# A decoder block on one core: the position bias as straight-line code with one conditional behind it

## The chip, the cores and the metric

The kernel runs on one core of one Trainium2 chip. The metric is the device time of one execution in microseconds (us). The kernel before takes 893.34 us, the median of three runs (891.0 to 894.33). TensorE does the matmuls, VectorE and ScalarE the elementwise work, GpSimd some of it, and SyncE starts most transfers; ScalarE starts the others, from its own queue.

## The reference

The reference is one decoder block over 512 tokens of width 1024: sparse attention with a T5 position bias beside a retention branch, gated and merged, then a layer norm, a squared-ReLU MLP of width 4096 and a second layer norm. What matters here is the bias of the attention: each query row keeps the 128 best keys by an indexer's score, and the logits of 8 heads get a bias that depends only on the distance of the two positions, by 32 buckets.

```python
def t5_bucket(rel):
    n = jnp.maximum(rel, 0)
    max_exact = NUM_BUCKETS // 2
    nf = jnp.maximum(n, 1).astype(jnp.float32)
    large = max_exact + (jnp.log(nf / max_exact) / math.log(MAX_DISTANCE / max_exact)
                         * (NUM_BUCKETS - max_exact)).astype(jnp.int32)
    large = jnp.minimum(large, NUM_BUCKETS - 1)
    return jnp.where(n < max_exact, n, large)
...
        bias = rel_bias[t5_bucket(posb[:, :, None] - pos_g)]
        logits = (jnp.einsum('bqhd,bqkhd->bqhk', qb, k_g).astype(jnp.float32) * (dh ** -0.5)
                  + bias.astype(jnp.float32).transpose(0, 1, 3, 2))
```

`positions` is an input. In the data that is timed it is 0, 1, 2, ..., 511; a kernel has to hold for others too.

## The kernel before

Every large product is done in full precision by three TensorE passes over a high and a low part (`mm3`, L142 to L147). A weight unit of 256 x 512 numbers is loaded by SyncE (`load_unit`, L124, four buffers), ScalarE casts its high part (`split_hi`, L132, three buffers), VectorE subtracts to get the low part (`split_lo`, L139, three buffers), and `group` runs the matmuls of the unit, 24 for each of the main projections. Each of these instructions stands in the queue of its engine; within a queue the order is fixed when the program is built. The builder walks through `main`, and at each `yield` of `group` (every 12 matmuls) calls `tick`, which advances the small tasks that are woven in between: rotary tables, indexer, top-k (L560, L561, on VectorE), the loads of the bias and the addition of the mask to it (`bm_task`, L578, L580), attention (`attn_task`, L617 to L657), retention. A planner then orders the instructions of each straight stretch of the program; a conditional ends a stretch, on all engines.

The order of the main projections is: indexer (8 units of a smaller kind, 8 ticks), attention keys (ticks 9 to 16), queries (17 to 24), values (25 to 32), then retention queries and keys with the rotary evacuation (`rope_evac`, L670, L673), and the rest.

The bias is made in three steps. `bias_by_distance` (L349) makes a row `R8` in DRAM, 8 heads by 640 distances. `bias_even` (L367) copies it, for positions that go up by one, into a DRAM tensor `bd[j]` for each of four blocks of 128 queries, 128 shifted copies of a row in one transfer. `bm_task` reads tiles of `bd` from there. For other positions `bias_general` computes every bias from its distance: `bias_prep` (VectorE) and 32 `bias_task`s (one-hot tables on VectorE, 12 matmuls each, ScalarE, a transfer). `bias_tables` finds out which case it is, a number `uneven` (L310), and `bias` (L328) holds the conditional at L333. It is called twice, behind the keys with heads 0 to 3 and behind the queries with heads 4 to 7; only the second call has the other arm.

```python
        uneven = self.nc.values_load(self.uneven[0:1, 0:1])
        with tc.If(uneven == 0) as cmp:
            self.bias_even(hs)
        if hs.stop == H:
            with cmp.Else():
                self.bias_general()
            self.flags.add("bias")
```

Of the kernel before, what the change touches and what calls it, by code (L numbers as in the profile page):

```python
# [11 lines left out]
F32 = mybir.dt.float32  # L12
F32R = mybir.dt.float32r
BF16 = mybir.dt.bfloat16
# [5 lines left out]
P = 128  # L20
# [3 lines left out]
H = 8  # L24
# [35 lines left out]
class Build:  # L60
# [67 lines left out]
    def split_hi(self, i):  # L128
        if i >= len(self.units) or i in self.whi:
            return  # L130
        hi = self.w.tile([P, *self.units[i][1:]], F32R, tag="whi", name=f"whi{i}", bufs=3)
        self.nc.scalar.copy(hi, self.raw[i])  # L132
        self.whi[i] = hi

    def split_lo(self, i):
# [122 lines left out]
    def setup_small(self):  # L258
        nc, d, sm = self.nc, self.d, self.sm
        self.cst = sm.tile([P, 160], F32, name="cst")  # L260
        nc.sync.dma_start(self.cst, d["cst"])
        self.posq = sm.tile([P, 4], I32, name="posq")
        nc.sync.dma_start(self.posq, d["posq"])
        self.posn = sm.tile([P, 4], I32, name="posn")
        nc.sync.dma_start(self.posn, d["posn"])
        self.posk = self.alloc(dt=I32, name="posk")
        nc.sync.dma_start(self.posk, d["positions"].to_broadcast([P, S]))
        self.mhalf = sm.tile([P, 16], F32, name="mhalf")
        nc.vector.memset(self.mhalf, -0.5)
# [19 lines left out]
    def bias_tables(self):  # L289
# [5 lines left out]
        for i in range(3):  # L295
            nc.vector.tensor_copy(parts[:, i], rb[:, i])
            if i < 2:
                nc.vector.tensor_sub(rb[:, i + 1], rb[:, i], parts[:, i])
        self.rbd = sm.tile([P, 3, 4, H], BF16, name="rbd")
        nc.vector.memset(self.rbd, 0.0)  # L300
        for q in range(4):
            r = slice(32 * q, 32 * q + 32)
            nc.vector.tensor_copy(self.rbd[r, :, q, :], parts[r])
        step, odd = self.alloc(shape=(1, S), dt=I32, name="step"), self.alloc(shape=(1, S), name="odd")
        n = S - 1
        nc.gpsimd.tensor_tensor(step[:, :n], self.posk[0:1, 1:], self.posk[0:1, :n], op=OP.subtract)
# [18 lines left out]
        return bass.AP(tensor=t.tensor, offset=t.offset + h * (P * w + P) + q * w + P - 1,  # L325
                       ap=[[w, nq], [P * w + P, nh], [1, n]])

    def bias(self, hs):  # L328


        tc = self.tc
        uneven = self.nc.values_load(self.uneven[0:1, 0:1])
        with tc.If(uneven == 0) as cmp:  # L333
            self.bias_even(hs)
        if hs.stop == H:
            with cmp.Else():
                self.bias_general()
            self.flags.add("bias")

    def bias_general(self):  # L340
        run, todo = [], [self.bias_prep()] + [self.bias_task(j, G) for j in range(NS) for G in range(8)]
        while run or todo:
            if todo:
                run.append(todo.pop(0))
            for g in list(run):
                if next(g, self) is self:
                    run.remove(g)

    def bias_by_distance(self):  # L349

# [4 lines left out]
        for i, sl in enumerate((slice(0, S), slice(S, W))):  # L355
            n = sl.stop - sl.start
            nc.sync.dma_start(bk[i][:, :n], self.d["buckets"][:, sl].to_broadcast([P, n]))
            nc.vector.tensor_scalar(oh[i][:, :n], bk[i][:, :n], self.bucket, None, op0=OP.is_equal)
            ps = self.ps.tile([P, S], F32, tag="s", name="tps", bufs=3)
            for p in range(3):  # L360
                nc.tensor.matmul(ps[:H, :n], lhsT=self.rbd[:, p, 0, :], rhs=oh[i][:, :n],
                                 start=p == 0, stop=p == 2)
# [4 lines left out]
    def bias_even(self, hs):  # L367

        for j in range(NS):
            w = self.pitch(j) + 1  # L370
            row = self.R8[hs, S - P * (j + 1):S - P * (j + 1) + w]
            src = bass.AP(tensor=row.tensor, offset=row.offset, ap=[[0, P], row.ap[0], row.ap[1]])
            self.nc.scalar.dma_start(self.bd[j][hs, :P * w].rearrange("h (q w) -> q h w", q=P), src)

    def bias_prep(self):

        nc = self.nc
        self.nd = []
        for j in range(NS):
            K = P * (j + 1)  # L380
            dn = self.alloc(dt=I32, name="dn")
            nc.gpsimd.tensor_tensor(dn[:, :K], self.posq[:, j:j + 1].to_broadcast([P, K]),
                                    self.posk[:, :K], op=OP.subtract)
            nv = self.allocs(2, name="nv")
            n, v = nv[0][:, :K], nv[1][:, :K]
            nc.vector.tensor_scalar(n, dn[:, :K], 0.0, NMAX, op0=OP.max, op1=OP.min)
            nc.vector.tensor_scalar(v, n, 1.0, None, op0=OP.max)
            nc.scalar.activation(v, v, AF.Ln, scale=0.0625)
            nc.vector.tensor_scalar(v, v, 16 / math.log(8), -0.49, op0=OP.mult, op1=OP.add)
            nc.vector.tensor_scalar(v, v, MAGIC, MAGIC - 1, op0=OP.add, op1=OP.max)  # L390
            nc.vector.tensor_scalar(v, v, MAGIC - 1, None, op0=OP.subtract)
            nb = self.alloc(dt=BF16, name="nb")
            nc.vector.scalar_tensor_tensor(nb[:, :K], n, 15.0, v, op0=OP.min, op1=OP.add)
            nd = self.dr.tile([P, K], BF16, name=f"nd{j}")
            nc.sync.dma_start(nd, nb[:, :K])
            self.free(dn, nb, nv)
            self.nd.append(nd)
            yield

    def bias_task(self, j, G):  # L400

        nc = self.nc
        K, C = P * (j + 1), P * j + 16 * (G + 1)
        while len(self.nd) <= j:
            yield
        yield from self.need(4)
        st = self.allocs(2, shape=(P, 2, K), dt=BF16, name="bst")
        for i in range(2):
            src = self.nd[j][16 * G:16 * G + 16, :].rearrange("(q g) k -> q g k", q=4)
            src = src[:, 2 * i:2 * i + 2].rearrange("q g k -> q (g k)")  # L410
            nc.sync.dma_start(st[i].rearrange("p g k -> p (g k)"),
                              src[:, None, :].to_broadcast([4, 32, 2 * K]))
        yield
        yield
        oh = self.allocs(2, shape=(P, 2, C), dt=BF16, name="boh")
        for i in range(2):
            nc.vector.tensor_scalar(oh[i], st[i][:, :, :C], self.bucket, None, op0=OP.is_equal)
        self.free(st)
        yield
        ps = self.ps.tile([P, S], F32, tag="s", name="bps", bufs=3)  # L420
        for p in range(3):
            for g in range(4):
                nc.tensor.matmul(ps[32 * g:32 * g + 32, :C],
                                 lhsT=self.rbd[:, p].rearrange("p q h -> p (q h)"),
                                 rhs=oh[g // 2][:, g % 2, :], start=p == 0, stop=p == 2)
        self.free(oh)
        ev = self.alloc(name="bev")
        nc.scalar.copy(ev[:, :C], ps[:, :C])
        if C < K:
            nc.gpsimd.memset(ev[:, C:K], 0.0)  # L430
        yield
        nc.sync.dma_start(self.bias_at(j, 0, H, 16 * G, 16, K), ev[:, :K])
        self.free(ev)


    def rope_prep(self):
# [351 lines left out]
    def main(self):  # L788
# [23 lines left out]
        for k in range(8):  # L812
            if k < 2:
# [10 lines left out]
        nc.vector.tensor_scalar(self.mask[0], self.causal, -1e38, NEG, op0=OP.is_lt, op1=OP.mult)  # L824
        self.flags.add("mask0")
        self.queue([self.rope_prep()], delay=14)
        self.queue([self.bm_task(j, 2 * i + p) for i in range(4) for j in range(NS) for p in range(2)],
                   1.0, 32)

# [17 lines left out]
        tb = [(P * i, P) for i in range(4)]  # L847
        self.kaT = self.allocs(4, name="kaT")
        yield from self.group(4, xT, tb, ev_copy(self.kaT, 1.0, "ka"), True)
        self.bias(slice(0, 4))  # L850
        self.qaT = self.allocs(4, name="qaT")
        yield from self.group(4, xT, tb, ev_copy(self.qaT, 0.125, "qa"), True)
        self.bias(slice(4, 8))
        self.free(self.posk)

        self.va = [self.allocs(2, name="va") for _ in range(4)]
        for v in self.va:
# [3 lines left out]
        def ev_va(bi, ps):  # L861
# [225 lines left out]
def arrays_of(inp):  # L1087
# [29 lines left out]
    out["positions"] = pos[None]  # L1117
    posn = pos.reshape(4, P)
    out["posn"] = np.ascontiguousarray(posn.T)

    out["posq"] = np.ascontiguousarray(posn.reshape(4, 8, 4, 4).transpose(0, 1, 3, 2).reshape(4, P).T)
    out["rb4"] = np.tile(a("rel_bias"), (4, 1))
    for n in ("idx_k_ln_g", "idx_k_ln_b", "ln_mix_g", "ln_mix_b", "ln_ffn_g", "ln_ffn_b"):
        out[n] = a(n)
    return out
# [17 lines left out]
```

## Time and profile before

| | before |
|---|---|
| three runs, median (lowest to highest) | 893.34 us (891.0 to 894.33) |
| the profiled execution, its time | 893.39 us |
| its span, first to last instruction | 891.6 us |
| mean granted clock of TensorE, share of full speed | 0.985 |
| busy: TensorE, VectorE, ScalarE, GpSimd | 852.8, 497.5, 300.2, 119.4 us |
| TensorE without a matmul | 38.8 us (891.6 less 852.8) |
| bytes moved by transfers | 95.32 MB |

The profile is of one execution. Its views are the page (busy times, transfers, costliest groups), the waits (who waited for whom), windows (busy times in stretches of time), the timeline (instructions in order), and the instructions of one source line. Times are from the start of the span. PE is TensorE, DVE VectorE, ACT ScalarE, POOL GpSimd, SP SyncE; a q behind the name is the engine's own queue, with its branches, semaphores and transfer issues. "issue" is time in which the engine waited for nothing that the profile shows.

### The profile page before, as it was taken

The page shows a single profiled execution, that of the slowest core. Times are in us where ns is not written, and L with a number is a line of the kernel's source. Part 1 is how long each engine was busy: PE and PEld are TensorE (multiplying, and loading weights), DVE is VectorE, ACT ScalarE, POOL GpSimd, SP SyncE. Part 2 cuts the span into 40 slices and gives each one's busy share as a digit, 9 for nine tenths or more (in the row PEclk, how much of TensorE's full clock was granted, in tenths as well). Part 3 has the DMA queues.
Part 4 walks back from the last instruction along what each step waited for, and adds up shares of the span by engine and source line. Part 5 has one row for each costly group of instructions (what it writes and reads, how often), then busy time and mean ns, then how long its engine had stood idle before and what let it go on. Part 6 is the DMA issues. An engine that isn't in the chain of part 4 may idle for free. (4 is left out here: it accounts for less than half of the span.)

```text
span 891.6 us, 11014 instructions
## 1 busy us (share of the span) xinstructions
PE 852.8 (96%) x4154; PEld 715.8 (80%) x4154; DVE 497.5 (56%) x973; ACT 300.2 (34%) x540; POOL 119.4 (13%) x135
## 2 busy tenths in 40 slices
PE   8996899799999999999999899999999999999996
PEld 7785788588877888888888689888888888888885
DVE  6787599943664466644256685344434433443447
ACT  4543426243454331313223313344114411441300
POOL 0000423411120021161022053000000000000002
PEclk9998899999999999999999999999999999999999
DMA  8876753233243021253433520233333333323302
GB/s 260 195 192 139 163 163 103 62 97 114 59 130 107 2 95 48 71 201 104 145 94 119 189 71 1 71 95 94 95 95 98 99 96 106 98 95 94 119 1 94
DMA packets 35994, 95.32 MB, mean 107 GB/s; under 512 B 4304, under 2 KB 12120, under 8 KB 35936
## 3 DMA queue, kind: packets, MB, share of 16 engines
q1 hardware_dynamic: 31712, 87.24, 31.4%
q10 hardware_dynamic: 4224, 7.32, 4.6%
q8 instruction: 34, 0.56, 0.3%
q14 instruction: 24, 0.20, 0.1%
HBM read 92.43 MB, written 9.44 MB: 114 GB/s over the span
## 5 line engine op out<-in xcount | busy, mean ns | idle before, releaser
L139 DVE TENSOR_TENSOR wlo<-raw,whi 128x1024 fp32r<-128x1024 f32 (+1 forms) x132 | 161.0, 1220 | 242.6 <-ACT whi L132 242.0
L132 ACT CAST whi<-raw 128x1024 fp32r<-128x1024 f32 (+1 forms) x132 | 134.0, 1016 | 332.7 <-PE mps L146 159.4
L147 PE MATMUL mps<-whi,xTl 128*128 128x512 f32 (+1 forms) x256 | 96.9, 388 | 10.9 <-issue 10.9
L145 PE MATMUL mps<-whi,xTh 128*128 128x512 f32 (+1 forms) x256 | 96.2, 394 | 6.7 <-DVE rt L673 5.7
L146 PE MATMUL mps<-wlo,xTh 128*128 128x512 f32 (+1 forms) x256 | 98.9, 389 | 0.0
L146 PE MATMUL mps<-x1Tl,whi 128*128 128x512 f32 x224 | 87.2, 389 | 0.0
L146 PE MATMUL mps<-wlo,hidh 128*128 128x512 f32 x224 | 87.2, 389 | 0.0
L145 PE MATMUL mps<-x1Th,whi 128*128 128x512 f32 x224 | 87.2, 389 | 0.0
L147 PE MATMUL mps<-whi,hidl 128*128 128x512 f32 x224 | 87.2, 389 | 0.0
L145 PE MATMUL mps<-whi,hidh 128*128 128x512 f32 x224 | 87.0, 389 | 0.0
L147 PE MATMUL mps<-x1Th,wlo 128*128 128x512 f32 x224 | 87.0, 389 | 0.0
L145 PE MATMUL mps<-xTh,whi 128*128 128x512 f32 x192 | 75.9, 396 | 1.5 <-ACT whi L132 1.5
L147 PE MATMUL mps<-xTh,wlo 128*128 128x512 f32 x192 | 74.5, 391 | 1.0 <-DVE wlo L139 1.0
L146 PE MATMUL mps<-xTl,whi 128*128 128x512 f32 x192 | 75.3, 392 | 0.0
L147 PEld LDWEIGHTS mps<-whi,xTl 128*128 128x128 f32 x256 | 48.6, 192 | 20.2 <-issue 11.3
L145 PEld LDWEIGHTS mps<-whi,xTh 128*128 128x128 f32 x256 | 48.5, 192 | 17.0 <-DVE rt L673 5.4
L146 PEld LDWEIGHTS mps<-wlo,xTh 128*128 128x128 f32 x256 | 49.2, 193 | 8.6
L254 POOL TENSOR_SCALAR rstd<-lnmv 128x1 f32<-128x1 f32 x8 | 5.1, 643 | 372.9 <-DVE lnmv L774 372.8
L146 PEld LDWEIGHTS mps<-wlo,hidh 128*128 128x128 f32 x224 | 42.1, 188 | 8.8
L147 PEld LDWEIGHTS mps<-x1Th,wlo 128*128 128x128 f32 x224 | 42.1, 188 | 8.7
L146 PEld LDWEIGHTS mps<-x1Tl,whi 128*128 128x128 f32 x224 | 42.1, 188 | 8.7
L147 PEld LDWEIGHTS mps<-whi,hidl 128*128 128x128 f32 x224 | 42.1, 188 | 8.7
(207 smaller groups left out, 1500.7 us busy)
## 6 DMA issues: line engine op xcount, KB each, us to landing
raw<-wp SPq DMA_DIRECT2D x136, 512.0 KB, 3.7
bd<-R ACTq DMA_DIRECT2D x2, 1278.0 KB, 28.1
xraw<-xT SPq DMA_DIRECT2D x8, 256.0 KB, 4.6
bm<-bd SPq DMA_DIRECT2D x8, 256.0 KB, 2.7
xn<-x SPq DMA_DIRECT2D x8, 256.0 KB, 4.5
out<-out SPq DMA_DIRECT2D x8, 256.0 KB, 2.0
bd<-R ACTq DMA_DIRECT2D x2, 1022.0 KB, 23.3
bm<-bd SPq DMA_DIRECT2D x8, 192.0 KB, 3.1
```

The costliest lines, as they stand in the source:

```text
L132: self.nc.scalar.copy(hi, self.raw[i])
L139: self.nc.vector.tensor_sub(lo, self.raw.pop(i), self.whi[i].bitcast(F32))
L145: mm(out, lhsT=a[0], rhs=b[0], start=first, stop=False)
L146: mm(out, lhsT=a[0], rhs=b[1], start=False, stop=False)
L147: mm(out, lhsT=a[1], rhs=b[0], start=False, stop=last)
L254: nc.gpsimd.tensor_scalar(t[:, :n], var, EPS, None, op0=OP.add)
```

## The change

The two conditionals go. `bias_even` becomes a task of the planner with a delay of 12 ticks: it writes the copies always, for four heads at a time, so that there are eight transfers, with two ticks between them; each is queued on ScalarE behind the cast (`split_hi`) that was traced last. Behind the value projection, once all eight are traced, `bias_other` holds the one conditional: if the positions are uneven, `bias_general` writes the bias over the copies. It is new: for each block VectorE computes bucket numbers, compares them with each of 32 buckets and adds the bucket's bias for each of 8 heads; TensorE has no part in it. The conditional is given `preferred_fallthrough_block=False`. The load of `posq` goes, and `rbd` loses a dimension. The arrays made on the host lose `posq` and gain `rbf`, which only `bias_general` reads.

```diff
-        self.nc.scalar.copy(hi, self.raw[i])
+        self.last_hi = self.nc.scalar.copy(hi, self.raw[i]).ins
...
-        self.posq = sm.tile([P, 4], I32, name="posq")
-        nc.sync.dma_start(self.posq, d["posq"])
...
-        self.rbd = sm.tile([P, 3, 4, H], BF16, name="rbd")
+        self.rbd = sm.tile([P, 3, H], BF16, name="rbd")
         nc.vector.memset(self.rbd, 0.0)
-        for q in range(4):
-            r = slice(32 * q, 32 * q + 32)
-            nc.vector.tensor_copy(self.rbd[r, :, q, :], parts[r])
+        nc.vector.tensor_copy(self.rbd[:32], parts[:32])
...
-    def bias(self, hs):
...
+    def bias_even(self):
+        yield from self.wait("R8")
+        for j in range(NS):
+            w = self.pitch(j) + 1
+            for h in range(0, H, 4):
+                row = self.R8[h:h + 4, S - P * (j + 1):S - P * (j + 1) + w]
+                src = bass.AP(tensor=row.tensor, offset=row.offset, ap=[[0, P], row.ap[0], row.ap[1]])
+                with self.tc.issue_after(self.last_hi):
+                    self.nc.scalar.dma_start(
+                        self.bd[j][h:h + 4, :P * w].rearrange("h (q w) -> q h w", q=P), src)
+                yield
+                yield
+        self.flags.add("even")
+
+    def bias_other(self):
         uneven = self.nc.values_load(self.uneven[0:1, 0:1])
-        with tc.If(uneven == 0) as cmp:
-            self.bias_even(hs)
-        if hs.stop == H:
-            with cmp.Else():
-                self.bias_general()
-            self.flags.add("bias")
+        with self.tc.If(uneven, preferred_fallthrough_block=False):
+            self.bias_general()
+        self.flags.add("bias")
 
     def bias_general(self):
...
+        nc = self.nc
+        V = nc.vector
+        rb = self.alloc(name="rbb")
+        nc.sync.dma_start(rb[:, :32 * H], self.d["rbf"].to_broadcast([P, 32 * H]))
+        for j in range(NS):
+            K = P * (j + 1)
...
+            V.scalar_tensor_tensor(n, n, 15.0, v, op0=OP.min, op1=OP.add)
+            acc = self.allocs(H, name="acc")
+            for b in range(32):
+                if b:
+                    V.tensor_scalar(v, n, float(b), None, op0=OP.is_equal)
+                for h in range(H):
+                    w, a = rb[:, b * H + h:b * H + h + 1], acc[h][:, :K]
+                    if b == 0:
+                        V.tensor_scalar(a, n, 0.0, w, op0=OP.is_equal, op1=OP.mult)
+                    else:
+                        V.scalar_tensor_tensor(a, v, w, a, op0=OP.mult, op1=OP.add)
+            for h in range(H):
+                nc.sync.dma_start(self.bias_at(j, h, 1, 0, P, K).rearrange("q h k -> q (h k)"), acc[h][:, :K])
...
         self.queue([self.rope_prep()], delay=14)
+        self.queue([self.bias_even()], delay=12)
...
         yield from self.group(4, xT, tb, ev_copy(self.kaT, 1.0, "ka"), True)
-        self.bias(slice(0, 4))
         self.qaT = self.allocs(4, name="qaT")
         yield from self.group(4, xT, tb, ev_copy(self.qaT, 0.125, "qa"), True)
-        self.bias(slice(4, 8))
-        self.free(self.posk)
...
         yield from self.group(4, xT, range(4), ev_va, False)
+        yield from self.wait("even")
+        self.bias_other()
+        self.free(self.posk)
```

## Rows read from the trace of the kernel before

**Rows 1.** The page, part 1: busy time of each engine.
```profile
PE 852.8 (96%) x4154; PEld 715.8 (80%) x4154; DVE 497.5 (56%) x973; ACT 300.2 (34%) x540; POOL 119.4 (13%) x135
```

**Rows 2.** Waits of TensorE: line, releaser: us in total, times, longest.
```profile
PE mps L147 <- issue: 10.9, 1, 10.9
PE mps L145 <- DVE rt L673: 5.7, 2, 4.9
...
PE mps L145 <- ACT whi L132: 1.5, 1, 1.5
PE mps L147 <- DVE wlo L139: 1.0, 1, 1.0
```

**Rows 3.** Windows from 81.25 to 179.05 us.
```profile
core 0: us, PE busy (x) PEld busy (x) DVE busy (x) ACT busy (x) POOL busy (x), PEclk, DMA share, GB/s
81.25:92.14 10.89, 0.00 (x1) 0.01 (x1) 4.58 (x10) 1.05 (x1) 1.45 (x3) 0.60 1.03 199
92.14:97.13 4.99, 4.99 (x12) 3.93 (x13) 0.00 (x0) 0.00 (x0) 2.80 (x6) 0.50 1.03 160
97.13:170.76 73.63, 72.87 (x350) 60.30 (x348) 67.18 (x143) 34.77 (x81) 23.16 (x29) 1.00 0.43 129
170.76:175.70 4.94, 0.00 (x0) 0.00 (x1) 4.86 (x11) 1.63 (x4) 2.34 (x2) 0.99 0.00 0
175.70:179.05 3.35, 3.35 (x8) 2.68 (x9) 3.13 (x7) 0.00 (x0) 2.73 (x2) 0.50 0.00 0
```

**Rows 4.** Line 333, TensorE and VectorE: durations ns min/median/max, first and last start.
```profile
L333 PEldq COMPARE_BRANCH  x4: 63/142/10640, 29.2 to 81.4; - x4
...
L333 DVEq COMPARE_BRANCH  x4: 47/50/55, 28.5 to 77.0; - x4
```

**Rows 5.** Timeline of ScalarE, VectorE, SyncE: start, us, engine, instruction [idle before, releaser].
```profile
29.34 5.29 ACTq L373 DMA_DIRECT2D bd<-R  x4
...
73.81 1.05 ACT L132 CAST whi<-raw 128x1024 fp32r<-128x1024 f32 x1 [0.54 <-PE mps L146]
...
98.41 1.05 ACT L132 CAST whi<-raw 128x1024 fp32r<-128x1024 f32 x1 [16.08 <-PE mps L147]
...
99.50 1.23 DVE L139 TENSOR_TENSOR wlo<-raw,whi 128x1024 fp32r<-128x1024 f32 x1 [13.51 <-ACT whi L132]
...
101.38 1.76 SPq L578 DMA_DIRECT2D bm<-bd  x4
...
112.26 0.28 DVE L621 CUSTOM_DVE_ANT_0 lg<-qkps,bm 128x128 f32<-128x128 f32 x1
```

**Rows 6.** Timeline of TensorE at the two clocks.
```profile
93.16 0.63 PE L146 MATMUL mps<-wlo,xTh 128*128 128x512 f32 x1
93.58 0.63 PE L147 MATMUL mps<-whi,xTl 128*128 128x512 f32 x1
...
97.98 0.39 PE L147 MATMUL mps<-whi,xTl 128*128 128x512 f32 x1
98.21 0.39 PE L145 MATMUL mps<-whi,xTh 128*128 128x512 f32 x1
```

**Rows 7.** Waits of SyncE's queue and VectorE, in the form of rows 2.
```profile
SPq L124 <- DVE wlo L139: 535.7, 108, 35.9
...
SPq L333 <- SPq L333: 17.1, 2, 16.6
...
DVE iqT L490 <- ACT iqT L489: 4.3, 1, 4.3
...
DVE sc L561 <- DVEq L333: 0.7, 1, 0.7
```

**Rows 8.** The page, parts 3 and 6: transfer queues; issues, us to landing.
```profile
q1 hardware_dynamic: 31712, 87.24, 31.4%
q10 hardware_dynamic: 4224, 7.32, 4.6%
...
raw<-wp SPq DMA_DIRECT2D x136, 512.0 KB, 3.7
```

More of the change, by code (lines that the diff above doesn't have):

```diff
@@ L326, in bias_at @@
                        ap=[[w, nq], [P * w + P, nh], [1, n]])
-    def bias(self, hs):
-        tc = self.tc
-        uneven = self.nc.values_load(self.uneven[0:1, 0:1])
-        with tc.If(uneven == 0) as cmp:
-            self.bias_even(hs)
-        if hs.stop == H:
-            with cmp.Else():
-                self.bias_general()
-            self.flags.add("bias")
-    def bias_general(self):
[L341 to L347, printed above, removed]
+    def bias_even(self):
[11 more added lines that the diff above has]
+        self.flags.add("even")
@@ new lines, in bias_other @@
+    def bias_other(self):
+        uneven = self.nc.values_load(self.uneven[0:1, 0:1])
+        with self.tc.If(uneven, preferred_fallthrough_block=False):
+            self.bias_general()
+        self.flags.add("bias")
+    def bias_general(self):
+        nc = self.nc
[4 more added lines that the diff above has]
+            K = P * (j + 1)
+            dn = self.alloc(dt=I32, name="dn")
+            nc.gpsimd.tensor_tensor(dn[:, :K], self.posn[:, j:j + 1].to_broadcast([P, K]),
+                                    self.posk[:, :K], op=OP.subtract)
+            nv = self.allocs(2, name="nv")
+            n, v = nv[0][:, :K], nv[1][:, :K]
+            V.tensor_scalar(n, dn[:, :K], 0.0, NMAX, op0=OP.max, op1=OP.min)
+            V.tensor_scalar(v, n, 1.0, None, op0=OP.max)
+            nc.scalar.activation(v, v, AF.Ln, scale=0.0625)
+            V.tensor_scalar(v, v, 16 / math.log(8), -0.49, op0=OP.mult, op1=OP.add)
+            V.tensor_scalar(v, v, MAGIC, MAGIC - 1, op0=OP.add, op1=OP.max)
+            V.tensor_scalar(v, v, MAGIC - 1, None, op0=OP.subtract)
+            V.scalar_tensor_tensor(n, n, 15.0, v, op0=OP.min, op1=OP.add)
[11 more added lines that the diff above has]
+                nc.sync.dma_start(self.bias_at(j, h, 1, 0, P, K).rearrange("q h k -> q (h k)"), acc[h][:, :K])
+            self.free(dn, nv, acc)
+        self.free(rb)
@@ L360, in bias_by_distance @@
             for p in range(3):
-                nc.tensor.matmul(ps[:H, :n], lhsT=self.rbd[:, p, 0, :], rhs=oh[i][:, :n],
+                nc.tensor.matmul(ps[:H, :n], lhsT=self.rbd[:, p], rhs=oh[i][:, :n],
                                  start=p == 0, stop=p == 2)
@@ L365, in bias_by_distance @@
         self.free(bk, oh, ev)
[L367 to L433, printed above, removed]
@@ L436, in rope_prep @@
+        self.flags.add("R8")
     def rope_prep(self):
@@ L1119, in arrays_of @@
     out["posn"] = np.ascontiguousarray(posn.T)
-    out["posq"] = np.ascontiguousarray(posn.reshape(4, 8, 4, 4).transpose(0, 1, 3, 2).reshape(4, P).T)
     out["rb4"] = np.tile(a("rel_bias"), (4, 1))
+    out["rbf"] = np.ascontiguousarray(a("rel_bias").reshape(1, -1))
     for n in ("idx_k_ln_g", "idx_k_ln_b", "ln_mix_g", "ln_mix_b", "ln_ffn_g", "ln_ffn_b"):
```

## The prediction

> **What bounds the kernel now.** I read the page first: TensorE is busy for 852.8 us of a span of 891.6 us [rows 1]. So a change pays only where TensorE stands still or runs at the lower clock. The waits of TensorE come next: the longest is one idle stretch of 10.9 us ahead of a matmul of L147, put down to "issue", which means that no buffer and no engine was late; the next is 4.9 us on VectorE's rotary evacuation, L673 [rows 2]. The windows by stage place both. [...] The branch instructions name the cause. Line 333 is the old bias's conditional, and one of TensorE's four branches there took 10640 ns, from 81.4, where its median is 142 ns and VectorE's longest 55 ns [rows 4]. By the code the arm that is not taken holds 32 tasks of 12 matmuls, each with a weight load: 768 TensorE instructions that have to be jumped over. VectorE's part of that arm is 92 operations. While TensorE's branch stands, the DMA share is 1.03 [rows 3]: transfers of the bias are in flight.
>
> TensorE is not alone in the hole. VectorE sits idle for 13.51 us, until 99.50, for the cast of the next weight unit, and the cast on ScalarE for 16.08 us, for a weight buffer that TensorE has not released [rows 5]. After that, from 97.13 to 170.76, VectorE is busy for 67.18 of 73.63 us, 91%; at the end of this stage TensorE runs nothing for 4.94 us, waiting for VectorE, and then 3.35 us at clock 0.50 [rows 2, 3]. VectorE is close to being the limit there, and that decides what a delay on VectorE costs.
>
> **The change, part by part.**
>
> *TensorE's jump goes.* The copies stand in the straight line now, and the one conditional left holds no TensorE instruction, so TensorE has nothing to jump over. That returns the idle 10.89 us. It returns the low clock as well: matmuls start 0.42 us apart at 93.16 and 0.23 us apart at 97.98 [rows 6], so of the 4.99 us from 92.14 to 97.13 the part lost is 4.99 x (1 - 0.23/0.42) = 2.3 us. Together 13.2 us. Does another wait take the stall's place? Weights don't: TensorE waits for a cast or a low part for 1.5 and 1.0 us in the whole run [rows 2], and SyncE's loads run ahead until they wait for a free buffer (108 times behind the splits of L139) [rows 7]. VectorE doesn't by itself: its own hole of 13.51 us goes with TensorE's, so the two keep their distance.
>
> *The new conditional.* It stands, in program order, behind the value projection; each engine still loads the flag and branches, and the semaphores of the skipped arm are still made good. Half of TensorE's four branches at the old two took 142 ns or less, the shortest 63 ns [rows 4]: I take nothing for TensorE. VectorE's wait at the old one was 0.7 us [rows 7]; I take +0.7 us, since VectorE has little slack there. The upper end is another matter: the arm to be skipped holds, by the code, 4 x (7 + 8 + 31 x 9) = 1176 VectorE instructions. If VectorE has to jump them, that costs between 0.05 us (92 jumped by VectorE) and 10.64 us (768 jumped by TensorE) [rows 4]. In count it is nearest to TensorE's; but the new flag asks that the false arm be the one that follows, and the copies should have landed by then (below). In the sum I take 0, and the rest is a rival.
>
> [...]
>
> *SyncE.* At the join of the old conditional it held for 17.1 us in all [rows 7]: it waits there for loads of its own that are still in flight, behind the bias transfers, and what is queued behind it on SyncE, weight loads and the loads of the bias by the masks, waits too. The new join has the same kind of hold. I cost it at nothing; its cover is the loads that run ahead, and how far that cover goes is the second rival.
>
> *The copies.* The bytes are the same, the times are not. Before, there were two bursts of four on ScalarE's queue, the first from 29.34 on [rows 5], the second behind the cast at 73.81. Now one copy comes every two ticks of the planner (one weight unit: 24 matmuls x 0.23 = 5.4 us, somewhat more with the work between), each behind the cast that was traced last. The first is due at tick 13, in the third unit of the key projection, behind the cast one unit ahead, near 31 us; the eighth behind the cast that ran at 73.81 [rows 5]. The queue's 7.32 MB take 4.6% of the span of 16 engines, 41 us; a weight unit of 0.52 MB takes 280 us x 0.52/87.24 = 1.7 us [rows 8]. 41 us and eight units, 14 us, from 31 us on: the last copy lands near 86 us. The first use is far off: the first softmax step on VectorE (L621), at 112.26 [rows 5], would stand near 99.
>
> *ScalarE.* The first burst held its queue for 5.29 us [rows 5] and so kept VectorE waiting 4.3 us for the indexer's cast [rows 7]. Now eight issues of the same kind are spread. Nothing of this is on TensorE's path, since casts run ahead; it may let the top-k on VectorE start some 4 us earlier, the third rival. One small load (`posq`) and three small VectorE copies go. I take 0.
>
> Sum against the profiled execution, 893.39 us (a span of 891.6 and 1.8 around it), which is 0.05 from the median, 893.34: 893.4 - 10.9 - 2.3 + 0.7 = 880.9, so 881. The order of instructions is planned anew over one longer block; I estimate that at 4 us either way, the size of the second-largest gap [rows 2]: 877 to 885.
>
> **The rivals.**
>
> 1. *VectorE jumps.* The 1176 instructions cost it a fetch: between 3.7 us, a load's landing [rows 8], and 10.64 us. Against the long end: the copies have landed by then, while TensorE's branch had a DMA share of 1.03 beside it. For it: VectorE is 91% busy in the stage that follows, so the delay goes nearly in full to TensorE's gap at 170. Time: 881 + 3.7 to 10.6 = 885 to 892.
> 2. *The bias comes late.* SyncE holds until the last copy has landed; then come the bias loads (3.7 us to land) and GpSimd's add. With L621 due near 99, copies that land after 94 block VectorE. If they land at 101, when the first bias load could leave before [rows 5], it costs 7 us: 888. For it: the DMA share is about 1 while copies run [rows 3]. Against it: the sum of 86.
> 3. *VectorE gets ahead.* If the freed 4.3 us reach the top-k, the gap of 4.94 us goes and with it the low clock behind it (3.35 x 0.47 = 1.6 us) [rows 3]: 881 - 6.5 = 874.5.
> 4. *Slower.* VectorE's jump takes two fetches, each like TensorE's: 21.3 us at the join. The 6.5 us that VectorE is idle in the stage hide a part, say 4; TensorE then stands still and gets the low clock behind it (2.3 us). 881 + 21.3 + 2.3 - 4 = 900.6. It decides from a hold of about 17 us on VectorE. Against it: no engine has shown two such fetches.
> 5. *It doesn't do it.* TensorE's branch misses again at its new place: 893. Against it: there is no TensorE instruction to jump.
>
> **How the numbers follow.** Forecast 0.52; rival 1 0.15, rival 2 0.09, rival 3 0.13, rival 4 0.07, rival 5 0.04. A change within 0.5% (4.5 us) is about what a measurement of this kernel can tell from none, so "faster" ends at 888.9. Faster: 0.52 + 0.13 + 0.08 of rival 1 + 0.05 of rival 2 = 0.78. Same: what is left of these two and rival 5, 0.15. Slower: rival 4, 0.07. The range takes in rival 3 below, and above it most of rivals 1 and 2: 873 to 890.
>
> **What would show it.** In the changed profile: TensorE's waits without the 10.9 us of "issue"; a granted clock of 1.00 throughout from 80 to 100 us; TensorE's branches at the new conditional all below 0.3 us; no wait of 13.5 us of VectorE for a cast; the first L621 near 99 us; the copies landed and the first bias load issued before 94 us. I am wrong if TensorE's gap at the end of the top-k grows past 8 us (rivals 1 and 4, told by the length of VectorE's branch) or if VectorE waits there for a bias tile (rival 2).

## The result, and the profile after

The changed kernel takes 882.06 us, the median of four runs (880.98 to 883.25), against 893.24 for the kernel before beside it: a ratio of 0.9878, 95% interval [0.9856, 0.9901], 11.2 us less. The forecast was 881. Its profiled execution took 881.98 us with a span of 880.2. Line numbers have moved: the conditional is L343, the copies L334, the bias loads L545, mask and bias L547, the top-k L527 and L528, the first softmax step L588, the rotary evacuation L637 and L640.

The page's busy times, with the queue of the copies:

```profile
PE 851.5 (97%) x4154; PEld 714.9 (81%) x4154; DVE 503.6 (57%) x970; ACT 300.2 (34%) x540; POOL 116.0 (13%) x135
...
q10 hardware_dynamic: 4224, 7.32, 3.5%
```

TensorE's idle time is 880.2 - 851.5 = 28.7 us, where it was 38.8 [rows 1]. The windows, with the columns of rows 3:

```profile
70.00:180.00 110.00, 100.39 (x458) 81.92 (x456) 94.99 (x198) 44.47 (x100) 28.11 (x32) 0.95 0.44 127
...
81.25:97.13 15.88, 15.88 (x72) 13.15 (x71) 14.75 (x33) 5.11 (x9) 0.00 (x0) 1.00 0.74 236
...
122.85:125.81 2.96, 0.00 (x0) 0.03 (x1) 2.96 (x8) 1.59 (x4) 0.63 (x2) 1.00 0.25 47
126.98:130.40 3.42, 3.42 (x9) 2.65 (x9) 3.42 (x8) 0.00 (x0) 2.80 (x4) 0.50 0.16 54
166.01:170.37 4.36, 0.01 (x2) 0.00 (x1) 4.24 (x12) 1.63 (x4) 0.94 (x2) 0.72 0.22 60
170.37:174.77 4.40, 4.40 (x10) 3.46 (x11) 3.21 (x7) 0.00 (x0) 2.92 (x3) 0.50 0.00 0
```

Where TensorE stood from 81.25 to 92.14 and then ran at clock 0.50 [rows 3], it now runs throughout at 1.00. But two gaps stand later, at 122.85 and at 166.01, each with a stretch at clock 0.50 behind it. The first is new; the second is the old one of 4.94 us at the end of the top-k. In the 110 us from 70 to 180, 458 matmuls start; this count is used below to compare kernels.

The waits (line, releaser: us in total, times, longest) and the branches at the conditional (ns min/median/max, first and last start):

```profile
PE mps L145 <- DVE rt L640: 7.3, 2, 4.4
PE mps L145 <- ACT inat L801: 3.7, 1, 3.7
...
PE qkps L584 <- DVE qk L563: 2.1, 1, 2.1
...
DVE sc L528 <- issue: 3.2, 1, 3.2
...
SPq L343 <- SPq L343: 2.3, 2, 1.9
```

```profile
L343 SPq COMPARE_BRANCH  x2: 38/44/49, 101.5 to 104.4; - x2
L343 DVEq COMPARE_BRANCH  x2: 51/53/55, 104.2 to 104.7; - x2
...
L343 PEldq COMPARE_BRANCH  x2: 85/136/187, 105.1 to 105.3; - x2
```

TensorE's "issue" wait of 10.9 us is gone and its branches take 85 to 187 ns. VectorE has an "issue" wait instead, 3.2 us, right behind its branch. The branch itself reads 55 ns: what VectorE's jump costs here is seen in the hole behind it and not in the branch's duration. The timeline (start, us, engine, instruction, idle before, releaser):

```profile
83.12 1.05 ACT L132 CAST whi<-raw 128x1024 fp32r<-128x1024 f32 x1 [5.94 <-PE mps L147]
86.75 1.05 ACT L132 CAST whi<-raw 128x1024 fp32r<-128x1024 f32 x1 [2.57 <-PE mps L147]
...
103.87 0.69 DVE L527 MAX8 m<-sc 128x8 f32<-128x512 f32 x1
107.72 0.09 DVE L528 MATCH_VALUE_LOAD sc<-m,sc 128x8 f32 x1 [3.16 <-issue]
...
109.63 4.19 DVE L563 TENSOR_TENSOR qk<-qaT,qk 64x512 fp32r<-64x512 f32 x1
...
115.86 0.69 DVE L563 TENSOR_TENSOR qk<-qaT,qk 64x512 fp32r<-64x512 f32 x1
...
120.52 0.29 DVE L588 CUSTOM_DVE_ANT_0 lg<-qkps,bm 128x128 f32<-128x128 f32 x1
...
100.56 0.33 SPq L124 DMA_DIRECT2D raw<-wp  x1
104.69 3.24 SPq L545 DMA_DIRECT2D bm<-bd  x7
...
104.72 3.89 POOL L845 MEMSET qrT<- 64x512 f32 x8 [76.15 <-DVEq L343]
108.59 4.69 POOL L547 TENSOR_TENSOR bm<-bm,mk 128x128 f32<-128x128 f32 x6
...
120.86 0.40 ACT L598 ACTIVATE pr<-lg,nm 128x128 f32<-128x128 f32 x1 [9.55 <-DVE nm L588]
...
121.26 1.04 ACT L132 CAST whi<-raw 128x1024 fp32r<-128x1024 f32 x1
```

The first two casts are those that stood on either side of the stall; in the kernel before, the first of them is this one:

```profile
81.28 1.05 ACT L132 CAST whi<-raw 128x1024 fp32r<-128x1024 f32 x1
```

Three things are to be seen. The casts of these two successive weight units are 3.63 us apart where they were 17.13 apart, at 81.28 and 98.41 [rows 5 has the second]: 13.5 us regained. VectorE's hole is 3.16 us. And behind the conditional all starts late and in bunches: bias loads from 104.69, GpSimd's memsets ahead of its first addition, a subtraction of 4.19 us that else takes 0.69 (TensorE's 2.1 us at L584 are a wait for it), and ScalarE waiting 9.55 us for the softmax with a weight cast queued behind.

During VectorE's hole, 104.56 to 107.72, the transfers hold one packet of the instruction queues:

```profile
q14 instruction: 1, 0.01, 1.2%
```

By the times of the packets in the traces it is the same in every long hole of VectorE behind a branch, here and in the runs below: in each of the six above 3 us (3.16, 3.34, 3.55, 6.38, 6.81, 13.12) a packet of q14 ends 1.1 to 1.7 us before VectorE goes on. In none of the five under 2 us (0.69, 0.70, 0.71, 0.98, 1.63) does one end. TensorE's hole in the kernel before, 81.25 to 92.14, holds three packets of the instruction queues: two of q14, which end by 88.06, and one of q8, which ends at 90.59, 1.55 us before TensorE goes on:

```profile
q8 instruction: 1, 0.02, 0.8%
q14 instruction: 2, 0.02, 0.4%
```

### The profile page after: what moved, and what is told of

Its sections match the earlier page's. It is cut to its first block, busy times and chain, and to the rows that moved or that the text cites. A ratio compares the mean times of both kernels' runs of the same rounds, so it can differ in the third digit from the quotient of the medians.

```text
span 880.2 us, 10991 instructions
## 1 busy us (share of the span) xinstructions
PE 851.5 (97%) x4154; PEld 714.9 (81%) x4154; DVE 503.6 (57%) x970; ACT 300.2 (34%) x540; POOL 116.0 (13%) x135
## 4 chain that ended last, share of the span: by engine, by line
PE 90%; DVE 5%; DMA 2%; issue 1%; ACT 1%; SPq 0%; POOLq 0%; POOL 0%; DVEq 0%; ACTq 0%
PE mps L145 27%; PE mps L146 27%; PE mps L147 27%; PE yT L618 1%; DMA raw<-wp 1%; DMA xraw<-xT 1%; PE ptps L609 1%; PE inps L672 1%; PE ops L681 1%; DVE wlo L139 1%; DVE qk L563 1%; PE ops L684 1%; PE kvps L691 1%; DVE sc L528 1%; ACT whi L132 0%
## 5 line engine op out<-in xcount | busy, mean ns | idle before, releaser
L147 PE MATMUL mps<-xTh,wlo 128*128 128x512 f32 x192 | 74.8, 393 | 0.0
L145 PEld LDWEIGHTS mps<-x1Th,whi 128*128 128x128 f32 x224 | 42.0, 188 | 8.7
L145 PEld LDWEIGHTS mps<-whi,hidh 128*128 128x128 f32 x224 | 42.0, 188 | 8.7
## 6 DMA issues: line engine op xcount, KB each, us to landing
bd<-R ACTq DMA_DIRECT2D x2, 1022.0 KB, 13.1
```

What stands on the lines that cost most here:

```text
L145: mm(out, lhsT=a[0], rhs=b[0], start=first, stop=False)
L147: mm(out, lhsT=a[1], rhs=b[0], start=False, stop=last)
```

## The experiments

Two questions were left. Which part of the change removed the stall? And what does the new conditional still cost? The theory at the outset ("A"): little of it is VectorE's jump; the rest is the cut through the plan and the late bias behind it. Where an arm is cut or left out below, a part of the bias for other positions is what is missing.

### Which part removed the stall

**The new arm in the old place.** The kernel before with its two conditionals and its copies inside them; only the arm for other positions is the new one, on VectorE.

```diff
     def bias_general(self):
-        run, todo = [], [self.bias_prep()] + [self.bias_task(j, G) for j in range(NS) for G in range(8)]
...
+            for b in range(32):
+                if b:
+                    V.tensor_scalar(v, n, float(b), None, op0=OP.is_equal)
...
```

> The kernel before with one edit: the arm that is not taken in the second conditional is the new one, 1175 VectorE instructions and one TensorE branch, in place of 768 TensorE instructions. Both conditionals and the two bursts of four copies stay where they were. Theory (the stall is TensorE's jump over its own instructions): TensorE's idle 10.9 us ahead of L147 goes, the clock stays at 1.00 there, and VectorE has a hole of 3 to 10 us behind its branch instead; time 880 to 885 us. Rival (the stall comes from the burst of copies, whatever the arm holds): TensorE still stands for about 11 us, 891 to 894 us.

Measured 891.02 us, ratio 0.9975 [0.9949, 1.0001]: next to nothing, outside the theory's 880 to 885 and with the time of the rival, though not by its mechanism. TensorE's branches, VectorE's timeline, the copies' queue during VectorE's hole (the last number is its share of the 16 engines), and TensorE's longest wait:

```profile
L333 PEldq COMPARE_BRANCH  x4: 63/134/185, 29.5 to 64.6; - x4
```

```profile
78.22 0.29 DVE L517 TENSOR_TENSOR sc<-sc,causal 128x128 f32<-128x128 f32 x1 [13.12 <-issue]
```

```profile
q10 hardware_dynamic: 1110, 1.55, 88.2%
```

```profile
PE mps L146 <- DVE wlo L139: 7.9, 1, 7.9
```

TensorE no longer jumps, but VectorE does, for 13.12 us beside the copies, and TensorE then waits 7.9 us for a low part. The stall changes engines.

**The old arm in the new place.** The changed kernel with the 768 TensorE instructions back in its arm.

```diff
+        run, todo = [], [self.bias_prep()] + [self.bias_task(j, G) for j in range(NS) for G in range(8)]
...
-        rb = self.alloc(name="rbb")
```

> The changed kernel with the old arm: the conditional at its new place holds the 768 TensorE instructions that the kernel before jumped over, and few of VectorE. The copies have landed there (they have by 95 us, the branch comes at 105). Theory A (the price of the jump is a fetch that waits behind transfers): TensorE stands for 3 to 5 us, and VectorE's hole of 3.2 us is gone; time 880 to 885. Theory B (the price belongs to TensorE and to the size of the arm): TensorE stands for 10 to 11 us and gets the low clock behind it; time 889 to 894.

Measured 882.95 us, 0.9884 [0.9847, 0.9921]: no different from the changed kernel.

```profile
L347 PEldq COMPARE_BRANCH  x2: 90/1932/3775, 105.4 to 109.2; - x2
```

```profile
PE mps L146 <- DVE m L565: 4.0, 1, 4.0
```

Here TensorE jumps again, and it takes 3.78 us where it took 10.64 [rows 4]; its gap there is 4.03 us long. (The profile puts the gap down to a step of VectorE, which ended at 112.62; the branch, begun at 109.21, ended later, at 112.98.) Taken together: at the new place, where the copies have landed, a jump is 3.8 us and not 10.6 on TensorE, 3.2 and not 13.1 on VectorE. So the place mattered more than which engine jumps. What makes the place dear is probably what else is being transferred: the copies' queue takes 85% and 88% of the transfer engines during the two long jumps, and nothing during the short ones. But place and copies change together in these runs, and none took the copies away at the old place.

**Two bursts.** The changed kernel with its copies in two bursts of four, as before.

```diff
-        self.queue([self.bias_even()], delay=12)
...
+        self.bias_even(slice(0, 4))
...
+        self.bias_even(slice(4, 8))
```

> The changed kernel with one part undone: the eight copies are issued in two bursts of four, behind the key and the query projection, each still behind the cast traced last. Theory (the spacing is worth nothing, because weights are loaded far ahead): within 2 us of the changed kernel's 882.1. Rival (the spacing carries part of the gain, by the loads that no longer queue behind a burst): slower by 4 us or more, with waits of TensorE or of casts for raw loads between 75 and 105 us, or with bias loads that leave later than 104.7.

Measured 882.07 us, 0.9882 [0.9841, 0.9923], with the same order of instructions on every compute engine. The spacing of the eight copies is worth nothing that these runs can tell.

### What the new conditional costs

**No conditional.** The path for other positions is left out.

```diff
-        uneven = self.nc.values_load(self.uneven[0:1, 0:1])
-        with self.tc.If(uneven, preferred_fallthrough_block=False):
-            self.bias_general()
         self.flags.add("bias")
```

> The changed kernel without its conditional: the part of the program for uneven positions is left out, which the timed data never takes. It measures what the new conditional still costs. Theory (VectorE's hole of 3.2 us at its jump, the bias loads that leave together behind the join and the two TensorE gaps of 2.1 and 3.0 us that follow are its price): faster by 3 to 7 us, 875 to 879. Rival (all of that is hidden, and the gaps come from the order of VectorE's work): within 2 us of 882.1.

Measured 871.21 us, 0.9764 [0.9728, 0.98]: the conditional costs 11 us. The page, the window, the first bias loads and TensorE's wait for the rotary evacuation:

```profile
PE 845.3 (98%) x4154; PEld 711.5 (82%) x4154; DVE 499.0 (58%) x970; ACT 300.9 (35%) x540; POOL 118.5 (14%) x135
```

```profile
70.00:180.00 110.00, 108.30 (x529) 90.43 (x528) 97.39 (x211) 49.69 (x117) 27.01 (x26) 1.00 0.48 145
```

```profile
86.38 0.90 SPq L542 DMA_DIRECT2D bm<-bd  x2
```

```profile
PE mps L145 <- DVE rt L637: 0.8, 1, 0.8
```

The profiled spans differ by 880.2 - 866.6 = 13.6 us (this execution is the fastest of the run's four). Of this TensorE's idle time is 28.7 - 21.3 = 7.4: its wait for the rotary evacuation falls from 7.3 to 0.8 us, and the 2.1 us behind the slow subtraction are gone. Its busy time, for the same 4154 matmuls, is the rest, 851.5 - 845.3 = 6.2: the granted clock is 1.00 throughout the window here, and of the changed kernel's stretches at 0.50 those from 126.98, 167.94 and 280.58 us are missing. VectorE's hole of 3.16 us can't be the whole of it.

**An arm of 94 VectorE instructions** (2 buckets of 32), the conditional at the same instruction of every engine; TensorE's 4154 matmuls, and the instructions of the other compute engines, run in the same order as in the changed kernel.

```diff
-            for b in range(32):
+            for b in range(2):
```

> The changed kernel with its arm cut from 1175 VectorE instructions to 94 (two buckets of 32, so the other positions' bias is left out); the conditional stays at the same instruction of each engine, behind 506 instructions of TensorE and 221 of VectorE. Theory A (VectorE's jump over the long arm is only the smaller part of the 11 us that the conditional costs; the rest is the cut that it makes through the plan: bias loads and scores can't leave before it): VectorE's 3.2 us hole shrinks to under 1 us, the bias loads still leave from about 104 us, first scores' matmul near 112, time 878 to 881. Rival B (the jump, and what it does to VectorE's later work, is the price): 871 to 875.

Measured 880.96 us, 0.9871 [0.9828, 0.9914].

```profile
105.99 0.09 DVE L528 MATCH_VALUE_LOAD sc<-m,sc 128x8 f32 x1 [0.70 <-DVEq L343]
...
118.31 0.29 DVE L588 CUSTOM_DVE_ANT_0 lg<-qkps,bm 128x128 f32<-128x128 f32 x1
```

The hole is 0.70 us in place of 3.16, the first softmax step 2.2 us earlier, the time 1.1 us less with intervals that overlap. At this place VectorE's jump is worth about 1 us, and most of the 11 has another cause.

**The conditional eight units earlier,** behind the query projection, with the long arm and then with the 32 buckets as a hardware loop (every path is kept; the loop itself is not entered with the timed positions).

```diff
         yield from self.group(4, xT, tb, ev_copy(self.qaT, 0.125, "qa"), True)
+        yield from self.wait("even")
+        self.bias_other()
```

```diff
-            for b in range(32):
...
+            with self.tc.For_i(0, 32, 1) as b:
+                V.tensor_copy(w8, rb[:, bass.ds(b * H, H)])
+                V.tensor_scalar(v, n, 0.0, None, op0=OP.is_equal)
+                V.tensor_scalar(n, n, 1.0, None, op0=OP.subtract)
```

> The changed kernel with the conditional one group of projections earlier (behind 381 instructions of TensorE in place of 506), its arm unchanged at 1174 VectorE instructions. Theory A (the price is the late cut): the bias loads leave near 90 us in place of 104.7, the bunch on GpSimd comes before attention, time 873 to 879 although VectorE still jumps. Rival B (the jump is the price, and it grows beside the copies, which end near 86 us): VectorE's hole is 5 to 13 us, time 883 to 890. Rival C (place has no effect): 882.

> The same earlier place, and the arm's 32 buckets as a hardware loop, so that it still computes every bias and holds some 150 VectorE instructions. Theory A: no hole of VectorE above 1 us, bias loads from about 88 us, time 871 to 876. If it comes out with the run of the long arm at this place, the jump costs nothing there; if it is at 882, neither place nor length matters and the join itself is the price.

Measured 885.55 us, 0.9904 [0.9873, 0.9934], and 885.74 us, 0.9918 [0.9891, 0.9944]: equal, and by their medians 3.5 and 3.7 us slower than the changed kernel, though the intervals overlap a little. Both expectations of theory A (873 to 879, 871 to 876) failed. The long arm, VectorE's timeline, waits and ScalarE's timeline, then VectorE's timeline of the loop:

```profile
86.08 0.29 DVE L531 TENSOR_SCALAR mk<-sc 128x256 bf16<-128x256 f32 x1 [6.81 <-issue]
```

```profile
PE mps L145 <- ACT whi L132: 2.1, 1, 2.1
PE mps L146 <- DVE wlo L139: 1.8, 1, 1.8
...
SPq L343 <- SPq L343: 17.5, 1, 17.5
```

```profile
92.64 0.62 ACT L560 CAST qk<-qaT 64x512 fp32r<-64x512 f32 x1 [10.13 <-SPq L343]
...
94.44 2.94 ACT L132 CAST whi<-raw 128x1024 fp32r<-128x1024 f32 x3
```

```profile
80.82 0.29 DVE L531 TENSOR_SCALAR mk<-sc 128x256 bf16<-128x256 f32 x1 [1.63 <-issue]
```

The order is the same in the two on every compute engine, VectorE's hole 6.81 and 1.63 us, the time the same: here the jump is covered. What covers it is SyncE, held 17.5 us (17.4 in the loop) at the conditional, from 74.8 to 92.2, until the last copies have landed (the copies' queue moves its last packets after 91.5). It doesn't reach TensorE by late weights: it reaches it by ScalarE, whose first cast for the attention behind the conditional (L560) waits 10.13 us for SyncE. Three weight casts stand behind it in ScalarE's queue and then run back to back, without a wait for a load; TensorE waits for a cast and a low part, 2.1 and 1.8 us near 93 to 98 us. That is the hold that the prediction costed at nothing, at a place where it decides. Why that cast depends on SyncE no run shows; its tile may take a slot that the arm uses.

**A short arm between.** An arm of 25 instructions for the last block alone; the planner then moves the conditional to 18 TensorE instructions behind the place of the last two.

```diff
-        for j in range(NS):
+        for j in (NS - 1,):
...
-            for b in range(32):
+            for b in range(2):
```

> The changed kernel with an arm of 25 VectorE instructions that touches the last quarter of the bias alone (the other positions' bias is left out); the planner then puts the conditional as soon as the copies allow, behind 399 instructions of TensorE. Theory A: as the loop at its earlier place, 871 to 876, no hole of VectorE. Rival: the wait for the last copy holds SyncE's queue and the weight loads behind it, a gap of TensorE over 5 us near 90 us, time over 880.

Measured 874.73 us, 0.9803 [0.9755, 0.9851]. SyncE is held again (branches from 78.9 to 90.1), but nothing on ScalarE, VectorE or TensorE waits for it, and no gap of TensorE follows. So the hold had no fixed price either: the place of the conditional in program order decided what waited behind it. What let it move was the tiles: the full arm takes fresh ones for each block, and these come free late; the next two runs, with one set, stand at the same place.

**Long arm and loop at that place,** complete, on one set of tiles.

```diff
+        dn = self.alloc(dt=I32, name="dn")
+        nv = self.allocs(2, name="nv")
+        acc = self.allocs(H, name="acc")
         for j in range(NS):
             K = P * (j + 1)
-            dn = self.alloc(dt=I32, name="dn")
...
-            acc = self.allocs(H, name="acc")
```

> The changed kernel with its arm complete (1177 VectorE instructions) but on one set of tiles for all four query tiles; so the planner puts the conditional as soon as the copies are issued, behind 399 instructions of TensorE, where the arm of 25 gave 874.7. Copies are still landing there. Theory A (a jump over a long arm waits for an instruction fetch behind the copies): VectorE's hole is 5 to 13 us and TensorE waits for weights, 879 to 888. Rival E (VectorE's hole is hidden, as it was one group earlier, where holes of 6.8 and 1.6 us gave the same time): 874 to 877.

> The same place as the run before, the arm complete, its 32 buckets as a hardware loop (16 VectorE instructions in each body). Theory A: no hole of VectorE above 1 us, bias loads from 91 us, time as with the arm of 25 instructions, 873 to 877: faster than the changed kernel by 5 to 9 us with every path kept. If it is at 880 or more, the length of the whole arm on all engines, and not VectorE's share, is the price.

Measured 879.31 us, 0.9845 [0.9822, 0.9869], and 873.63 us, 0.9774 [0.9754, 0.9795]. VectorE's timeline of the long arm, then of the loop, and the copies' queue during the loop's hole:

```profile
88.27 0.09 DVE L527 MATCH_VALUE_LOAD sc<-m,sc 128x8 f32 x1 [6.38 <-issue]
```

```profile
83.77 0.09 DVE L527 MATCH_VALUE_LOAD sc<-m,sc 128x8 f32 x1 [0.98 <-DVEq L343]
```

```profile
q10 hardware_dynamic: 98, 0.24, 86.9%
```

Again the order is the same in both, and in the run with 25 instructions too, and here nothing covers the jump: a hole of 6.38 against 0.98 us, and 0.9845 - 0.9774 = 0.0071, or 6.3 us (5.7 by the medians). Both times lie in theory A's ranges; but TensorE doesn't wait for weights in the long arm, as A had it, but for the rotary evacuation, 3.1 us against 0.8. The copies are under way in both holes, so that they alone didn't make the jump long here: it took the long arm as well. The loop keeps every path and is 8.4 us faster than the changed kernel by the medians. By its median it is the best version with both paths; the last run below is not told apart from it.

**Is it the late bias?** The kernel without a conditional, with its bias loads held behind four more weight loads.

```diff
-        uneven = self.nc.values_load(self.uneven[0:1, 0:1])
-        with self.tc.If(uneven, preferred_fallthrough_block=False):
-            self.bias_general()
+        self.n0 = self.loaded
...
         yield from self.wait("bias")
+        while self.loaded < self.n0 + 4:
+            yield
```

> The kernel without the conditional (the path for other positions is left out), with one thing more: the first seven bias loads are held in SyncE's queue behind the third weight load that they ran ahead of, so that they leave in one bunch near 102 us, as they do in the changed kernel (104.7), in place of 86 to 108 us. There is no branch and no hold. Theory A1 (of what the conditional costs, most is that bias loads and the attention behind them start late): 877 to 881, with gaps of TensorE near 123 and 166 us. Rival D (the price is the hold of SyncE's and GpSimd's queues at the conditional, or the plan cut in two): 870 to 874.

Measured 877.73 us, 0.9833 [0.9805, 0.9862], 6 us more than without the delay, inside theory A1's range. The timeline:

```profile
102.27 5.23 SPq L545 DMA_DIRECT2D bm<-bd  x8
...
107.93 0.29 DVE L588 CUSTOM_DVE_ANT_0 lg<-qkps,bm 128x128 f32<-128x128 f32 x1 [2.69 <-POOL bm L547]
```

But the gaps of TensorE near 123 and 166 us that A1 named beside the time don't come: its longest wait for the rotary evacuation is 1.2 us. And the delay also changes when the tasks behind it are traced, and so the order on the engines. The last run speaks against the theory that it seemed to bear out.

**The memsets first.** The changed kernel, with the eight memsets that GpSimd runs behind the conditional moved ahead of it.

```diff
+        self.qrT = [self.allocs(4, name="qrT") for _ in range(2)]
+        self.krT = self.allocs(4, name="krT")
+        for par in range(2):
+            for t in self.qrT[par]:
+                nc.gpsimd.memset(t[64 - 64 * par:128 - 64 * par], 0.0)
         yield from self.wait("even")
         self.bias_other()
```

> The changed kernel with the eight memsets of the retention queries' tiles, which stand behind the conditional in GpSimd's queue and run there for 3.9 us ahead of the first addition of bias and mask, moved ahead of it, where GpSimd has nothing to do. Nothing else of the work changes; the planner puts the conditional 12 TensorE instructions earlier. Theory A2 (what is left between the run with late bias loads, 877.7, and the changed kernel, 882.1, is attention that starts later still): the first addition runs near 105 to 106 us in place of 108.6, the first softmax step near 116 in place of 120.5, time 878 to 881. Rival: the attention is held by VectorE's own order and not by the bias, 882 or more.

Measured 874.66 us, 0.9794 [0.9769, 0.9818]: 7.4 us better than the changed kernel, below theory A2's 878 to 881, and not for the reason given. Timeline and waits:

```profile
108.29 0.09 DVE L528 MATCH_VALUE_LOAD sc<-m,sc 128x8 f32 x1 [3.55 <-issue]
...
119.52 0.29 DVE L588 CUSTOM_DVE_ANT_0 lg<-qkps,bm 128x128 f32<-128x128 f32 x1
```

```profile
PE mps L145 <- DVE rt L640: 2.4, 2, 1.6
```

VectorE's hole is still there (3.55 us), the bias loads leave later still (107.36), and the first softmax step is at 119.52, only 1.0 us before the changed kernel's. So neither the hole nor the late bias is what those 7 us are. What differs is the order of instructions: at 621 of TensorE's 4154 places another matmul stands. TensorE's waits for the rotary evacuation fall from 7.3 to 2.4 us, and no stretch from 70 to 180 us is at the lower clock.

## Why the prediction was right, point by point

| kernel | us | matmuls from 70 to 180 us, clock |
|---|---|---|
| before | 893.2 | 422, 0.92 |
| new arm in the old place | 891.0 | 434, 0.92 |
| long arm or loop, before the values | 885.6, 885.7 | 440, 443, 0.95 |
| old arm in the new place | 883.0 | 462, 0.95 |
| two bursts; changed | 882.1, 882.1 | 457, 458, 0.95 |
| arm of 94 | 881.0 | 474, 0.97 |
| long arm at the earlier place | 879.3 | 505, 0.98 |
| late bias, no conditional | 877.7 | 519, 1.00 |
| memsets first; short arm, loop at the earlier place | 874.7, 874.7, 873.6 | 517, 526, 526, 1.00 |
| no conditional | 871.2 | 529, 1.00 |

The time follows how many matmuls get through this one stretch, nearly in order. The count is of the one profiled execution; it shows where the time is lost and not why.

- *TensorE's jump, 13.2 us: right.* No "issue" wait, clock 1.00 from 81.25 to 97.13, branches under 0.2 us, and 13.5 us regained between two casts. That the place beside the copies made the jump long was only hinted at (the DMA share of 1.03); the old arm in the new place showed it.
- *The new conditional, +0.7 us on VectorE: mis-sized.* VectorE's hole is 3.16 us. Rival 1's mechanism happened, just under its lower end of 3.7 us. The reason that was given against its long end, that the copies have landed by then, held: beside copies the same jump took 13.12, 6.81 and 6.38 us. But its price was wrong: rival 1 passed the hole on to TensorE nearly in full, and the arm of 94 shows about 1 us. The packet in an instruction queue during the long holes and in none of the short ones fits a wait of VectorE for instructions, and 94 instructions showed no hole of this kind where 1175 did. What the prediction calls a fetch is in the traces no more than such a packet. That it lasts as long as a load's landing, 3.7 us, was the author's estimate: no run shows a fetch by itself, and the packet in the hole of 3.16 us took 0.60 us, from 105.77 to 106.37. Nor did the count of instructions alone set the price: the same 768 cost TensorE 10.64 us beside the copies and 3.78 us without them.
- *SyncE's hold at no cost: right here.* 2.3 us in all and no gap from it. It was luck of the place: eight units earlier the hold is 17.5 us, and TensorE pays, by ScalarE's casts. The prediction looked for the price in what SyncE has queued behind it; there it came by what ScalarE has queued.
- *The copies.* Predicted to land near 86 us; their queue moves its last packets after 90. They were in time, as 94 was the limit.
- *First bias load before 94 and first softmax step near 99: wrong.* They came at 104.69 and 120.52. The step that failed took the old place of the first softmax step less 13.2 us, and left out that the conditional moves: nothing behind it can be planned ahead of it, and it stood at 101.5 to 105.3 us. Without the conditional the bias loads leave at 86.38.
- *Planning anew, 4 us either way: the largest error hidden in the sum.* With identical work, moves of the conditional or of eight memsets gave 873.6 to 885.7 us. Before the stall was passed, the changed kernel was already behind: the cast at 73.81 [rows 5] is at 75.64 now, 1.8 us later, and TensorE's one start-up wait for the indexer (L801) is 3.7 us, with a stretch at clock 0.50 behind it, from 24.58 us.
- *Rival 3, 874.5 us by the gap at the end of the top-k vanishing.* Its condition came true in part: VectorE's wait for the indexer's cast fell from 4.3 [rows 7] to 1.0 us. The gap itself did not go in the changed kernel, where 4.36 us of it remain; nor did it grow past 8 us, the sign of rivals 1 and 4. It went in the two best versions, where the wait for the rotary evacuation falls to 2.4 and 0.8 us, and their 874.7 and 873.6 us are near its price.
- *The counts.* Of the seven operations that the prediction counts for each block one, the logarithm, is ScalarE's: by the code the new arm has 1172 on VectorE and the old one 88, not 1176 and 92. A weight unit is 24 x 0.23 = 5.5 us and not 5.4. Nothing hangs on these.

By the sum: 13.2 was expected for the stall and 0.7 was to be given back. Of the 13.5 regained, 1.8 had been lost ahead of the stall; the lead is 11.7 us at the cast of 86.75 (98.41 before) and 11.4 at the end. In between, VectorE's jump cost about 1 us and new gaps came, and the order of the rest made up for nearly all of that. The low clock shows the same: the stretch behind the stall went, others came, and TensorE's busy time fell by 852.8 - 851.5 = 1.3 us and not by 2.3. So the stall's mechanism was right, and that 12.5 forecast and 11.4 in the profiled executions lie so close is in part luck: they agree better than the parts do.

What stays open: which of the instructions that moved decides, and whether the copies themselves make a jump long. The two gaps of the changed kernel wait for the rotary evacuation on VectorE, and one weight cast stands behind a softmax on ScalarE; no run changed one of these alone.

## What to carry to other kernels

Look for a conditional's price on every engine that has instructions in the arm not taken, in the idle time behind the branch and in the branch itself: here it was 3.16 us behind a branch of 55 ns on VectorE, and 10.64 us in TensorE's branch. Beside the copies it was two to four times as large (6.38 to 13.12 us against 3.16 to 3.55 on VectorE, 10.64 against 3.78 on TensorE); an arm written as a loop cost 1.0 to 1.6 us even there. The conditional also fixed the order of all work around it: of its 11 us at the place of the changed kernel the jump was worth about 1. So try its place, and what stands directly behind it, before trimming the arm. When the work stays the same, count the matmuls that get through the stretch in question rather than single waits.

## What the hardware showed unexpectedly

The same jump has prices far apart: VectorE over some 1175 instructions 3.16 to 3.55 us with no copies in flight, 6.38 to 13.12 us beside them; TensorE over 768 instructions 3.78 and 10.64 us. VectorE over 92 or 94 instructions shows 0.7 us, over the loop arms 0.98 and 1.63 us beside the copies.

A VectorE subtraction was slow while GpSimd added: that of L563 took 4.19 us at 109.63, while GpSimd added masks from 108.59 to 113.28, and 0.69 us at 115.86 on the same shape. The 14 traces hold 336 subtractions of this shape (`qk`). All 251 that overlap no TENSOR_TENSOR of GpSimd took 0.66 to 0.69 us, 17 of them beside its memsets; of the 85 that overlap one, 57 took more than 0.75 us, up to 4.19. So the overlap was there in every slow one, and not every overlap was slow. No run took the overlap away alone.

SyncE was held at a conditional whose arm holds transfers until the transfers issued before it had landed: 17.4 and 17.5 us beside the copies in the two runs one group earlier, 10.2 to 10.7 in the three behind them, 2.3 us where only a weight load was under way. In the five runs with the conditional beside the copies its second branch comes 1.0 to 1.1 us behind the end of the copies' last packet.
